# Modulations of a two-layer token mixer: a 32-column zero-padded left operand, pieces of 512 columns over four column groups, one ScalarE copy out

## The chip, the cores and the metric

The kernel runs on one core of a Trainium2 chip. The metric is the device time of one execution in microseconds (us); the lower the better. Five engines work in parallel, each through its own list of instructions in order: TensorE (PE for its matmuls, PEld for its weight loads), VectorE (DVE), ScalarE (ACT), GpSimd (POOL) and SyncE (SP), which here issues the DMA transfers.

## What is computed

Two layers over 1024 latent tokens and 256 context tokens of width 1024. Each layer mixes tokens by four groups of heads (mLSTM, Hyena, retention, RWKV), then by a convolutional feed-forward network, and both are modulated: six vectors of 1024 for latents and six for context come from one matrix product with a 1024 x 6144 matrix.

```
for l in range(DEPTH):
    mod = jnp.split((silu_c @ ada_w[l] + ada_b[l])[:, None, :], 6, axis=-1)
    modc = jnp.split(silu_cc @ ada_w[l] + ada_b[l], 6, axis=-1)
    ...
    u = modulate(layer_norm(x), mod[0], mod[1])
    uc = modulate(layer_norm(xc), modc[0], modc[1])
    y, y_c = token_mixer(u, uc, p, ang, not last)
    x = layer_norm(DEEPNORM_ALPHA * x + mod[2] * y, ln1_g[l], ln1_b[l])
    u = modulate(layer_norm(x), mod[3], mod[4])
    f = conv_ffn(u, ffn_w_up[l], ffn_conv_w[l], ffn_conv_b[l], ffn_w_down[l])
    x = layer_norm(DEEPNORM_ALPHA * x + mod[5] * f, ln2_g[l], ln2_b[l])
    ...
```

The last layer needs no context output. All arithmetic is in 32-bit floats; the large projections split an operand into a high and a low part (`uh`, `ul`) and use three matmuls.

## The kernel before, in words

The program is written as one stream. A scheduler sorts each engine's instructions, and pools with named buffers (tags) decide what must wait: a tile that takes a tag's buffer waits for the last user of the tile that had it.

**Modulations.** `sc` [128, 8, 2] holds the two activated vectors, eight blocks of 128 rows, one column for latents and one for context. It is the left operand (the loaded weights, two columns), the columns of the matrix are the right one. `ada` does the first two modulations of layer 0 in the setup: tiles of 128 x 1024 in six buffers, and four column groups of the array, 256 columns each, whose two result rows stand at rows 0, 32, 64 and 96 of a PSUM bank. `ada_steps` does the other four of layer 0 and the first two of layer 1 during layer 0's scan, and the last four of layer 1 during its scan: pieces of 256 columns over two column groups (40 pieces, 24 and 16), each with four tiles of 256 rows, two buffers. The loads of the next piece are written behind the matmuls of one, so two of its four tiles are prefetched. `ada_out` copies the two rows of each column group to `ab` on DVE (L940), transposes `ab` on PE (L941) and adds the bias to give columns of `modc` (L944).

**The scan.** `rwkv` runs ten steps of a chunked scan, both directions at once. `rwkv_prep` makes a step's operands (L484 to L541), `rwkv_inverse` inverts its triangular blocks by substitution (a transpose into the tile LM at L550, then 31 rounds on POOL and DVE, L557 and L558), `rwkv_tail` finishes the inverse (L565 to L591), `rwkv_chain` carries the state (L601 to L637). In step s the order in the text is inverse(s+1), chain(s), for some steps `group_norm` of two finished token tiles, tail(s+1), prep(s+2). The norm runs for s = 1 (layer 0 alone) and s = 6 to 9: sums on DVE (L651 to L653), a Square on ScalarE into its work space `gq` (L654), a sum of it (L655), square root (L656), reciprocal (L657), a product on POOL into `gq` (L658), and a store of `gq` to `yw` (L659). mLSTM runs beside the scan, with the modulations' pieces between its steps; its `keys` loads have three buffers.

**The setup and the front.** `tile_backbone` computes two modulations, then normalizes and modulates the ten input tiles; `to_u` transposes them and splits them (`uh`, `ul`, the last part on POOL, L1010). `filters` builds Hyena's filters: a feature table `fft` (L268), two small layers with a Sine (L273 to L280), products with a window (L287 to L139). Then come the projections with Hyena between them, and retention, whose state chain `rSS` runs on POOL (L826, L827) before its last part on PE.

Of the kernel before, what the change touches and what calls it, by code (L numbers as in the profile page):

```python
# [20 lines left out]
def rwkv_consts():  # L21
# [6 lines left out]
    c['rwmask']=np.stack([mf,mb],1)          # [128,2,128]  # L28
# [10 lines left out]
def mr_consts():  # L39
# [3 lines left out]
    mk=np.zeros((128,2,128),np.float32)   # [j,dir,i]  # L43
    mk[:,0]=np.where(i[:,None]>i[None,:],-1e30,0); mk[:,1]=np.where(i[:,None]<i[None,:],-1e30,0)
    c['mmask']=mk
    # selection for token-major gathers: rows 0-7 wi, 32-39 wk, 64-71 em ; cols (dir,12)
# [5 lines left out]
    # decay broadcast: lhsT [8,(ft,dir),128]  # L52
# [5 lines left out]
    # block-diagonal rows [8 rows,(dir) , h', i]  # L58
# [26 lines left out]
def dft_consts(L):  # L85
    """two-stage real DFT of length 2L, n=128*n1+n2, k=R*m+r, R=2L/128"""
# [10 lines left out]
    F0=np.zeros((128,4,64))   # re0, reH, im0(row0=nyquist), imH  # L97
    F0[:,0]=np.cos(a0);F0[:,1]=np.cos(aH);F0[:,2]=-np.sin(a0);F0[:,2,0]=(-1.0)**n2;F0[:,3]=-np.sin(aH)
    I0=np.zeros((128,4,128))  # B0 from re, B0 from im, BH from re, BH from im
# [36 lines left out]
class Eng:  # L136
    """elementwise ops on DVE or on Pool"""
    def __init__(s,nc,pool): s.nc=nc; s.e=nc.gpsimd if pool else nc.vector; s.pool=pool
    def tt(s,out,a,b,op): s.e.tensor_tensor(out=out,in0=a,in1=b,op=op)  # L139
    def axpy(s,out,a,sc,b,op=ALU.add,tmp=None):   # a*sc op b  # L140
# [5 lines left out]
def stage_a(K,E,x,H,CW,ptag):  # L146
    """x: view [128,H,CW] (n1 = token tile). returns accessor re(r), im(r) for r=0..H"""
# [29 lines left out]
def fwd_slot(K,cs,dst_re,dst_im,slot,H,pre,pim,qre=None,qim=None):  # L177
    """matmuls of one slot: re part from (pre,pim), im part from (qre,qim)"""
# [10 lines left out]
def fft_conv(K,Ksp,x,out,H,CW):  # L189
    """x view [128,H,CW], Ksp DRAM AP [128,H,2,CW]; out callback(par(0/1), AP [128,H//2,CW] time values)"""  # L190
# [18 lines left out]
    BB=p.tile([128,2*H,CW],F32,tag="hE",name="BB")   # re r -> r (0..H), im r -> H+r  # L209
# [20 lines left out]
    # g: [128, comp(re,im), r, par, CW]  # L230
# [10 lines left out]
    # a4: even +re B4, odd -im B4  # L241
# [14 lines left out]
def hyena_filter(K,l,L,Ksp):  # L256
    """Ksp DRAM tile [2 order][128,H,2,256]"""
# [89 lines left out]
def seg_conv(k,dst,src,w,ctx=True):  # L347
    """three-tap conv of a padded feature-major tile; w = (prev, mid, next, bias) columns"""
# [18 lines left out]
def kparts(k,D,ft,t,kk):  # L367
    """keys (or normalized keys) to the groups of wrk: r | k of even heads, kk of odd ones | the other way round | kk"""
# [7 lines left out]
def rwkv_front(k,l,pv,pvr,last):  # L376
    """projections, token shift, key normalization, gate and bonus of the RWKV group"""
# [52 lines left out]
def rwkv(K,l,pv,last,p1,p2,p3):  # L430
    """Chunked scan, 64 tokens a chunk, both directions at once, two chunks of each a step.  Even heads keep (b,SA,S) on partitions
    0-63 and (k,V) on 64-127, odd heads the other way round."""
# [229 lines left out]
def mlstm(K,l,GT,last,side=None):  # L662
# [13 lines left out]
    def keys(t):  # L676
        kT=p.tile([128,2,128],F32,tag="mk",name="mk",bufs=3)
        nc.sync.dma_start(kT,K.D['mqk'][256:512,t*128:t*128+128].rearrange("(f p) t -> p f t",p=128))
        return kT
# [765 lines left out]
```

## Time and profile before

| what | us |
|---|---|
| runs of the kernel, median of 3 | 4327.93 |
| lowest and highest of them | 4318.99, 4331.74 |
| profiled execution, its span | 4332.8 |

The profiled execution's own time is given by its span alone; it lies 4.9 us above their median. The sums further down are made against the span and then taken to the runs. A count of busy time says what an engine did, and not that something waited for it; that is read from the timeline and from waits.

### The profile page before, as it was taken

Reading aid. Unit: us, or ns where it says so; the run is one execution under the profiler, and the core shown is the slowest. Engines: PE = TensorE matmul, PEld = TensorE weight load, DVE = VectorE, ACT = ScalarE, POOL = GpSimd, SP = SyncE. Lnnn points to the kernel's source line nnn. Section 1 sums busy time; section 2 is a strip of 40 time slices with the busy share of each in tenths; the row PEclk is TensorE's granted clock in tenths of the full one; section 3 lists DMA queues with packets and bytes.
Section 4 is the critical chain, followed back from the end, with each engine's and each line's share of the span. In section 5 each row is a group of like instructions: output and inputs, shape, how many; then the busy total and the mean of one; then the engine's idle time right before and its main releaser. Section 6 shows DMA issues by size and latency. Waiting matters only on the chain.

```text
span 4332.8 us, 65427 instructions
## 1 busy us (share of the span) xinstructions
PE 3976.9 (92%) x24976; PEld 3226.9 (74%) x24976; DVE 2644.4 (61%) x5384; ACT 1462.4 (34%) x2909; POOL 1094.6 (25%) x2204
## 2 busy tenths in 40 slices
PE   6999999689979999999996899997899879999997
PEld 3878877566657888888884688885666758888885
DVE  5656665889766544444448555776889664444446
ACT  4333233554344211111124443344544342112112
POOL 3230023566535000000033330033666340000004
PEclk6999999799989999999998999996899789999999
DMA  4235553444343111111113235553333331111112
GB/s 164 72 102 173 158 152 110 114 145 121 116 134 122 45 39 35 44 40 35 38 36 114 83 103 153 171 160 96 123 111 102 125 102 54 45 43 54 44 49 97
DMA packets 477141, 414.18 MB, mean 96 GB/s; under 512 B 48827, under 2 KB 443285, under 8 KB 474011
## 3 DMA queue, kind: packets, MB, share of 16 engines
q1 hardware_dynamic: 476826, 409.99, 31.1%
q8 instruction: 197, 3.23, 0.3%
q14 instruction: 118, 0.96, 0.1%
HBM read 323.65 MB, written 86.25 MB: 95 GB/s over the span
## 4 chain that ended last, share of the span: by engine, by line
PE 49%; DVE 11%; ACT 3%; issue 3%; DMA 3%; POOL 3%; SPq 0%; POOLq 0%; ACTq 0%; DVEq 0%
PE bank L1021 8%; PE bank L1023 8%; PE bank L1022 8%; PE dbank L1021 6%; PE dbank L1022 6%; PE dbank L1023 6%; DMA xt<-x 1%; DVE bst L983 1%; POOL ul L1157 1%; DVE facc L1204 1%; PE bank L186 1%; PE bank L187 0%; DMA wst<-in_w_out 0%; DVE G L530 0%; DVE XL L558 0%
## 5 line engine op out<-in xcount | busy, mean ns | idle before, releaser
L1021 PE MATMUL dbank<-uh,wh 128*128 128x512 f32 (+1 forms) x2120 | 764.4, 370 | 9.5 <-ACT tmpB L398 5.5
L1022 PE MATMUL dbank<-ul,wh 128*128 128x512 f32 (+1 forms) x2120 | 760.0, 368 | 0.0
L1015 DVE TENSOR_TENSOR wl<-wst,wh 128x1024 fp32r<-128x1024 f32 x146 | 188.9, 1295 | 491.4 <-ACT wh L1014 342.0
L1023 PE MATMUL dbank<-uh,wl 128*128 128x512 f32 (+1 forms) x2120 | 480.9, 367 | 0.0
L1021 PEld LDWEIGHTS dbank<-uh,wh 128*128 128x128 f32 x2120 | 401.1, 189 | 85.8 <-ACT ztok L1113 6.1
L1022 PEld LDWEIGHTS dbank<-ul,wh 128*128 128x128 f32 x2120 | 401.3, 189 | 68.4 <-issue 0.8
L1023 PEld LDWEIGHTS dbank<-uh,wl 128*128 128x128 f32 x2120 | 366.2, 188 | 70.6 <-issue 1.1
L1232 POOL MEMSET fz<- 128x1 f32 x132 | 7.3, 99 | 1441.4 <-DVE fc L1247 1441.2
L1021 PE MATMUL bank<-uh,wh 128*128 128x512 f32 (+1 forms) x920 | 337.8, 375 | 11.4 <-ACT uh L1009 11.4
L1263 DVE TENSOR_TENSOR facc<-facc,bank 128x512 f32<-128x512 f32 x324 | 222.1, 687 | 204.8 <-PE bank L1023 204.8
L1022 PE MATMUL bank<-ul,wh 128*128 128x512 f32 (+1 forms) x920 | 337.9, 375 | 4.1 <-POOL ul L1010 3.6
L1021 PE MATMUL bank<-wdh,gh 128*128 128x512 f32 x792 | 315.2, 400 | 19.2 <-DVE facc L1277 11.1
L1022 PE MATMUL bank<-wdl,gh 128*128 128x512 f32 x792 | 310.5, 392 | 3.4 <-DVE wdl L1015 3.4
L1023 PE MATMUL bank<-wdh,gl 128*128 128x512 f32 x792 | 248.7, 393 | 0.0
L1014 ACT ACTIVATE wh<-wst 128x1024 fp32r<-128x1024 f32 x146 | 154.6, 1059 | 226.2 <-PE dbank L1022 157.7
L1014 ACT ACTIVATE wdh<-wst 128x1024 fp32r<-128x1024 f32 x46 | 48.7, 1061 | 524.8 <-PE bank L1023 427.8
L557 POOL TENSOR_TENSOR lt<-LM,XL 128x48 f32<-128x48 f32 (+26 forms) x620 | 187.4, 302 | 121.7 <-ACT XL L551 51.1
L558 POOL TENSOR_TENSOR XL<-XL,lt 128x48 f32<-128x48 f32 (+26 forms) x620 | 205.9, 332 | 47.8
L1023 PE MATMUL bank<-uh,wl 128*128 128x512 f32 (+1 forms) x920 | 212.6, 373 | 0.0
L1021 PEld LDWEIGHTS bank<-uh,wh 128*128 128x128 f32 x920 | 176.2, 192 | 42.9 <-ACT uh L1009 12.2
L1022 PEld LDWEIGHTS bank<-ul,wh 128*128 128x128 f32 x920 | 176.0, 191 | 36.1 <-POOL ul L1010 4.3
L1021 PEld LDWEIGHTS bank<-wdh,gh 128*128 128x128 f32 x792 | 149.9, 189 | 59.2 <-DVE facc L1277 11.9
(480 smaller groups left out, 8283.0 us busy)
## 6 DMA issues: line engine op xcount, KB each, us to landing
wst<-in_ffn_w_up SPq DMA_DIRECT2D x88, 512.0 KB
adaw<-in_ada_w SPq DMA_DIRECT2D x160, 256.0 KB
wst<-in_w_in SPq DMA_DIRECT2D x58, 512.0 KB
wst<-in_ffn_w_down SPq DMA_DIRECT2D x46, 512.0 KB
df<-in_c_F SPq DMA_DIRECT2D x10, 1344.0 KB
xt<-x SPq DMA_DIRECT2D x26, 512.0 KB
df<-in_c_I SPq DMA_DIRECT2D x8, 1344.0 KB
rkk<-wrk SPq DMA_DIRECT2D x10, 1024.0 KB
```

The lines of the kernel that those rows point to most:

```text
L186: mm(dst_re,F[:,i],pre(slot),start=True,stop=False); mm(dst_re,F[:,i+1],pim(slot),start=False,stop=True)
L557: e.tensor_tensor(out=t_,in0=LM[:,j,j+1:32].unsqueeze(2).to_broadcast([128,n,m]),in1=X[h][:,j:j+1,0:m].to_broadcast([128,n,m]),op=A.mult)
L558: e.tensor_tensor(out=X[h][:,j+1:32,0:m],in0=X[h][:,j+1:32,0:m],in1=t_,op=A.add)
L983: for h in range(2): nc.vector.bn_stats(out=st[:,h],in_=x[h])
L1014: k.nc.scalar.activation(out=h,in_=st,func=ACTF.Copy)
L1015: k.nc.vector.tensor_tensor(out=lo,in0=st,in1=h,op=ALU.subtract)
L1021: mm(ps,lh,rh,start=(i==0),stop=False)
L1022: mm(ps,lh,rl,start=False,stop=False)
L1023: for i,((lh,ll),(rh,rl)) in enumerate(pairs): mm(ps,ll,rh,start=False,stop=(i==n-1 and more is None))
L1157: nc.gpsimd.tensor_tensor(out=k.ul[:,fs,c],in0=yT,in1=k.uh[:,fs,c],op=ALU.subtract)
L1204: e[0].tensor_tensor(out=y,in0=y,in1=g,op=ALU.mult)
L1263: else: tt(out=d,in0=d,in1=ps,op=ALU.add)
```

## The change

1. `ada_sc` makes a left operand of 32 columns a block: `sc` in the first two, zeros in the others. It is made in the setup and in each layer's scan. The matmuls write 32 rows of each column group, so all 128 rows of a bank where four groups are used.
2. `ada_steps` has pieces of 512 columns over four column groups (20 pieces, 12 and 8), each with eight tiles of 128 rows by 512 columns, still two buffers. A tile has 256 KB as before; there are 160 loads and 640 matmuls (1280 records) as before.
3. `ada_out` makes one ScalarE copy of all rows, and each piece has one transpose of 128 rows and one add.
4. RWKV's group norm takes its work space from the tag of LM, which has one buffer, instead of a tag of its own.
5. mLSTM's `keys` have two buffers instead of three.

```
-            group_norm(K,YF[:,sl],K.D['yw'].rearrange("(t p) c -> p t c",p=128)[:,sl],2,p2.tile([128,8,64],F32,tag="gq",name="gq"),"gnw")
+            group_norm(K,YF[:,sl],K.D['yw'].rearrange("(t p) c -> p t c",p=128)[:,sl],2,p2.tile([128,16,64],F32,tag="LM",name="gq"),"gnw")
...
-        kT=p.tile([128,2,128],F32,tag="mk",name="mk",bufs=3)
+        kT=p.tile([128,2,128],F32,tag="mk",name="mk",bufs=2)
...
+def ada_sc(k,pool):
+    s=pool.tile([128,8,32],F32,name="scz"); k.nc.gpsimd.memset(s,0.0); k.nc.gpsimd.tensor_copy(out=s[:,:,0:2],in_=k.sc)
+    return s
...
-    for j in range(G): nc.vector.tensor_copy(out=ab[32*j:32*j+2],in_=ps[32*j:32*j+2,0:n])
+    nc.scalar.activation(out=ab,in_=ps[:,0:n],func=ACTF.Copy)
...
-        for i in range(4): nc.tensor.matmul(b[32*i:32*i+2,0:256],k.sc[:,q],w[:,i*256:i*256+256],start=(q==0),stop=(q==7))
+        for i in range(4): nc.tensor.matmul(b[32*i:32*i+32,0:256],sc[:,q],w[:,i*256:i*256+256],start=(q==0),stop=(q==7))
...
-    nc=k.nc; units=[(l,g*1024+p*256) for l,g in todo for p in range(4)]; w={}
-    bias=ada_bias(k,todo,pool); ab=pool.tile([64,128],F32,name="ab"); nc.gpsimd.memset(ab,0.0)
+    nc=k.nc; units=[(l,g*1024+p*512) for l,g in todo for p in range(2)]; w={}
+    bias=ada_bias(k,todo,pool); ab=pool.tile([128,128],F32,name="ab"); sc=ada_sc(k,pool)
     def load(u):
         l,c0=units[u]; w[u]=[]
-        for h in range(4):
-            t=pool.tile([128,2,256],F32,tag="adaw",name="adaw",bufs=2); w[u].append(t)
-            nc.sync.dma_start(t,k.a['ada_w'][l,h*256:h*256+256,c0:c0+256].rearrange("(q p) c -> p q c",p=128))
+        for q in range(8):
+            t=pool.tile([128,512],F32,tag="adaw",name="adaw",bufs=2); w[u].append(t)
+            nc.sync.dma_start(t,k.a['ada_w'][l,q*128:q*128+128,c0:c0+512])
...
-                for j in range(2): nc.tensor.matmul(ps[32*j:32*j+2,0:128],k.sc[:,q],w[u][q//2][:,q%2,j*128:j*128+128],start=(q==0),stop=(q==7))
+                for j in range(4): nc.tensor.matmul(ps[32*j:32*j+32,0:128],sc[:,q],w[u][q][:,j*128:j*128+128],start=(q==0),stop=(q==7))
...
```

The scheduler sorts the changed program anew. Lines of the changed kernel from `ada_out` on are numbered six higher. DVE has 5278 instructions instead of 5386, ScalarE 2927 instead of 2911, PE 19342 instead of 19362.

DVE in layer 1's scan, around the transpose of inversion 8 (counted from 0) into LM. Before, its rows from the end of inversion 7 (the transpose of its result XL, L565) to that of LM:

```order
L565 STREAM_TRANSPOSE T_29958<-XL 128x128 [waits Pool_49]
L569 STREAM_TRANSPOSE XT_25622<-T_29958 32x4x32 [waits DVE_49]
L569 STREAM_TRANSPOSE XT_25622<-T_29958 32x4x32
L571 STREAM_TRANSPOSE AX<-T_29958 32x128
L569 STREAM_TRANSPOSE XT_25622<-T_29958 32x4x32
L940 COPY ab<-mbank 2x128 [waits PE_49]
L940 COPY ab<-mbank 2x128
L569 STREAM_TRANSPOSE XT_25622<-T_29958 32x4x32
L571 STREAM_TRANSPOSE AX<-T_29958 32x128
L550 STREAM_TRANSPOSE LM<-NB 128x1024 [waits Activation_49]
```

Of the change, the same engine's last rows ahead of the same transpose (the end of inversion 7, L565, stands 71 instructions ahead of it):

```order
L617 COPY VSA<-cbank 64x128 [waits Activation_49]
L655 TENSOR_REDUCE gn_r<-gq 128x8 [waits Activation_49]
L657 RECIPROCAL gn_r<-gn_r 128x8 [waits Activation_49]
L624 TENSOR_TENSOR SV<-cbank,rho 64x128 [waits PE_49]
L624 TENSOR_TENSOR SV<-cbank,rho 64x128
L657 RECIPROCAL gn_r<-gn_r 128x8 [waits Activation_49]
L785 TENSOR_TENSOR NUM<-NUM,mbank 128x260 [waits PE_49] x2
L624 TENSOR_TENSOR SV<-cbank,rho 64x128 [waits PE_49]
L624 TENSOR_TENSOR SV<-cbank,rho 64x128
L550 STREAM_TRANSPOSE LM<-NB 128x1024 [waits DMAHW1_49,Pool_49]
```

The chain of step 6 (SV, VSA) and its norm (gn_r) have moved ahead of the transpose, which now waits for a DMA and for POOL. The DMA is the store of gq.

SyncE's queue in the setup, around the load of the filter's feature table `fft`. Before, it stands behind two loads of input tiles, ahead of the window's (wn):

```order
L953 DMA adaw<-in_ada_w 128x1024 [waits DMAHW0_49,PE_49]
L1420 DMA xt<-in_x 128x1024 [waits DMAHW1_49]
L1420 DMA xt<-in_x 128x1024 [waits DMAHW2_49]
L268 DMA fft<-in_c_FT 33x1024 [waits DMAHW3_49]
L288 DMA wn<-in_c_WIN 128x128 [waits DMAHW4_49]
```

Of the change, it stands behind the last loads of the input (the two context tiles) and six of the biases:

```order
L1426 DMA xt<-in_ctx 128x1024 [waits DMAHW5_49,PE_49]
L1426 DMA xt<-in_ctx 128x1024 [waits DMAHW6_49,PE_49,Activation_49]
L884 DMA rowst<-in_ada_b 8x128 [waits PE_49]
L884 DMA rowst<-in_ada_b 8x128 [waits DMAHW0_49]
L884 DMA rowst<-in_ada_b 8x128 [waits DMAHW1_49]
L884 DMA rowst<-in_ada_b 8x128
L884 DMA rowst<-in_ada_b 8x128 [waits DMAHW3_49]
L884 DMA rowst<-in_ada_b 8x128 [waits DMAHW4_49]
L268 DMA fft<-in_c_FT 33x1024 [waits DMAHW6_49,DMAHW5_49,Pool_49]
```

The load of fft moved behind all ten input tiles and waits for POOL, which it did not before.

PE in layer 0's scan, where its first modulation piece begins. Before (adaw are the tiles of the matrix):

```order
L973 MATMUL mbank<-adaw,sc 2x128 [waits PE_49]
L973 MATMUL mbank<-adaw,sc 2x128 x3
L973 MATMUL mbank<-adaw,sc 2x128 [waits DMAHW5_49]
L973 MATMUL mbank<-adaw,sc 2x128 x3
L492 MATMUL pbank<-TWA,W_6721 128x128 [waits DMAHW7_49,Activation_49]
L492 MATMUL pbank<-TWA,W_6721 128x128 x2
```

Of the change, in the same place:

```order
L979 MATMUL mbank<-adaw,scz 32x128 [waits PE_49]
L979 MATMUL mbank<-adaw,scz 32x128 x3
L979 MATMUL mbank<-adaw,scz 32x128 [waits DMAHW5_49]
L979 MATMUL mbank<-adaw,scz 32x128 x3
L733 MATMUL mbank<-ident,mk 128x128 [waits DMAHW5_49,DVE_49,PE_49]
L733 MATMUL mbank<-ident,mk 128x128
L979 MATMUL mbank<-adaw,scz 32x128 [waits DMAHW1_49]
L979 MATMUL mbank<-adaw,scz 32x128 x3
L979 MATMUL mbank<-adaw,scz 32x128 [waits DMAHW2_49]
L979 MATMUL mbank<-adaw,scz 32x128 x3
```

A tile still feeds four matmuls, but now one block of rows in four column groups instead of two blocks in two; a piece has eight such groups of four, with other work between some of them.

## Rows read from the trace of the kernel before

**Rows 1.** The page: busy us, share of the span, instructions.
```profile
PE 3976.9 (92%) x24976; PEld 3226.9 (74%) x24976; DVE 2644.4 (61%) x5384; ACT 1462.4 (34%) x2909; POOL 1094.6 (25%) x2204
```

**Rows 2.** Table by stretch: us, then PE, PEld, DVE, ACT, POOL busy.
```profile
101.00:706.00 605.00, 592.31 (x3511) 501.51 (x3510) 369.81 (x773) 217.92 (x437) 116.71 (x244) 0.99 0.44 130
...
804.00:1127.00 323.00, 290.84 (x3407) 216.02 (x3408) 282.79 (x885) 152.76 (x440) 209.40 (x595) 0.88 0.39 117
```

**Rows 3.** Timeline of DVE and POOL, both scans: start us, us, operation.
```profile
804.50 1.95 DVE L550 STREAM_TRANSPOSE LM<-NB 128x1024 f32<-128x1024 f32 x1
...
908.21 1.95 DVE L550 STREAM_TRANSPOSE LM<-NB 128x1024 f32<-128x1024 f32 x1 [0.96 <-POOL lt L557]
...
908.25 0.20 POOL L558 TENSOR_TENSOR XL<-XL,lt 128x4 f32<-128x4 f32 x1
...
1126.92 1.97 DVE L550 STREAM_TRANSPOSE LM<-NB 128x1024 f32<-128x1024 f32 x1
...
3351.32 1.92 DVE L550 STREAM_TRANSPOSE LM<-NB 128x1024 f32<-128x1024 f32 x1
```

**Rows 4.** Groups by line: ns min/median/max, first and last start, forms.
```profile
L940 DVE COPY ab<-mbank x80: 236/282/284, 846.0 to 3335.4; 2x128 f32<-2x128 f32 x80
...
L614 ACT ACTIVATE U<-cbank x80: 250/278/307, 851.0 to 3412.4; 128x128 f32<-128x128 f32 x80
```

**Rows 5.** Timeline of PE (a scan piece, the setup), then groups by line.
```profile
840.60 0.61 PE L973 MATMUL mbank<-adaw,sc 128*2 128x128 f32 x8
...
8.86 4.45 PE L954 MATMUL dbank<-adaw,sc 128*2 128x256 f32 x40
...
L973 PE MATMUL mbank<-adaw,sc x1280: 271/272/421, 837.2 to 3331.8; 128*2 128x128 f32 x183
...
L1078 PEld LDWEIGHTS dbank<-uh,wh x24: 107/107/170, 95.4 to 106.3; 128*32 128x32 f32 x24
```

**Rows 6.** Waits of PE in layer 0's scan: us in total, times, longest.
```profile
PE mbank L973 <- DMA adaw<-in_ada_w: 6.0, 6, 2.4
```

**Rows 7.** The chain that ended last, in layer 1's scan.
```profile
3178.54 2.81 DMA adaw<-in_ada_w
```

**Rows 8.** Timeline of SyncE's queue: stores of RWKV's normalized output.
```profile
1151.51 0.37 SPq L659 DMA_DIRECT2D yw<-gq  x1
...
1209.77 0.37 SPq L659 DMA_DIRECT2D yw<-gq  x1
...
3379.56 0.39 SPq L659 DMA_DIRECT2D yw<-gq  x1
...
3421.20 0.36 SPq L659 DMA_DIRECT2D yw<-gq  x1
```

**Rows 9.** Timeline of ScalarE: the reader of the last store.
```profile
3423.43 1.06 ACT L1156 ACTIVATE uh<-yT 128x1024 fp32r<-128x1024 f32 x1 [3.61 <-DMA yw<-gq]
```

**Rows 10.** Timeline of POOL in the setup, then its groups by line.
```profile
100.67 2.40 POOL L1010 TENSOR_TENSOR ul<-tum,uh 128x1024 fp32r<-128x1024 f32 x1
...
L139 POOL TENSOR_TENSOR pq<-hh x16: 445/450/639, 83.0 to 105.2; 128x128 f32<-128x128 f32 x16
...
L139 POOL TENSOR_TENSOR hh<-hh,wn x8: 717/724/727, 81.6 to 103.0; 128x256 f32<-128x256 f32 x8
```

**Rows 11.** Groups by line, 0 to 101, then 101 to 706: busy, mean.
```profile
L287 PE MATMUL bank<-fw,fh 64*128 64x128 f32 x32 | 8.3, 438 | 2.2 <-ACT fh L280 2.2
...
L273 PE MATMUL bank<-fft,fw 33*64 33x512 f32 x4 | 3.7, 1071 | 1.4 <-DMA fft<-in_c_FT 1.4
...
L820 PE MATMUL bank<-rqkv,k 128*128 128x64 f32 x76 | 9.4, 269 | 0.0
```

**Rows 12.** Timeline of POOL: memsets and retention's state chain.
```profile
706.05 0.55 POOL L435 MEMSET W<- 128x512 f32 x1 [11.48 <-PE dbank L1023]
...
713.37 1.83 POOL L452 MEMSET XT<- 128x1024 f32 x2
...
724.61 1.86 POOL L827 TENSOR_TENSOR rSS<-rSS,rst 64x256 f32<-64x256 f32 x1
```

More of the change, by code (lines that the diff above doesn't have):

```diff
@@ L945, in ada_out, with ada @@
         in1=tv(bias[l,m][:,j0:j0+G*e].unsqueeze(2).to_broadcast([128,G*e,2])),op=ALU.add)
-def ada(k,l,g,pool,ab,loads,bufs,bias):
+def ada(k,l,g,pool,ab,loads,bufs,bias,sc):
     nc=k.nc; b=k.dbank()
@@ L1413, in tile_backbone @@
         loads=[]
-        ab=pa.tile([128,256],F32,name="ab"); nc.gpsimd.memset(ab,0.0)
+        ab=pa.tile([128,256],F32,name="ab"); sc=ada_sc(k,pa)
         bias=ada_bias(k,[(0,0),(0,1)],pa)
-        for g in range(2): ada(k,0,g,pa,ab,loads,6,bias)
+        for g in range(2): ada(k,0,g,pa,ab,loads,6,bias,sc)
         mc=k.modc[:,0:2].rearrange("p m j s -> p s m j")
```

## The prediction

> **What bounds the kernel now.** I read the page's busy shares first, since they name the engine that could gain: TensorE (PE) is busy 92% of 4332.8 us, VectorE (DVE) 61% [rows 1]. A share is a mean over stages, so the table by stretch comes next. From 101 to 706 us lie layer 0's projections, with PE busy 592.31 of 605 us; from 804 to 1127 its scan, where no engine is full: PE 290.84 and DVE 282.79 of 323 us [rows 2]. Layer 1's scan is alike and ends its tenth inversion after 3351.32 [rows 3]. The modulations run in the setup, before 101, and in both scans. What paces a scan is a chain: each of ten steps has an inversion, 62 short operations on GpSimd (POOL) and 30 on DVE, and the next one's first instruction, the transpose into LM, starts as the one before ends. The reader sees it in the timeline of the two engines: POOL's last operation of an inversion stands at 908.25, the next transpose at 908.21. Ten transposes from 804.50 to 1126.92 make a period of 35.8 us [rows 3].
>
> **The change, part by part.**
>
> *Copies, adds, transposes.* DVE's 80 copies of 0.282 us (22.6 us) become 20 copies on ScalarE [rows 4]; the nearest ScalarE row, a PSUM copy of 128x128, takes 0.278, so 5.6 us on an engine busy 152.76 of 323 [rows 2, 4]. The adds fall from 40 to 20, PE's transposes too. DVE loses some 26 us, three fifths in layer 0. These are rows of DVE and counted in the scan term below, not again.
>
> *TensorE.* In the scan eight records of a piece take 0.61 us, each 0.272: two column groups at once, so a pair starts every (0.61-0.27)/3 = 0.113 us. In the setup, where four groups are used already, 40 longer records end in 4.45 us, 0.111 each for twice the columns: far less than one record's length, so they do run side by side [rows 5]. The 1280 scan records then cost 320 x 0.113 = 36 us in place of 640 x 0.113 = 72; PE loses 22 us in layer 0, 14 in layer 1. The padded operand is 32 columns wide; a weight load of that width takes 0.107 us elsewhere [rows 5], less than the matmul beside it, on a queue busy 216.02 of 323 [rows 2]. I take nothing for PE, as it isn't in the chain of inversions; that it is, is a rival.
>
> *Refills.* A piece now has 8 tiles instead of 4, with two buffers: three pairs of loads behind the prefetched one instead of one, 60 rounds instead of 40. PE waited 6.0 us in six waits on them in layer 0's scan, which had 24 of the 40 [rows 6]: 0.25 a round, so **+5** for twenty more. Upper bound: nothing else stands between and each waits for a whole landing, 2.81 us in the chain that ended last [rows 7]: +56. The order puts scan matmuls between most rounds, which is nearer to the first. The Trainium skill, page "DMA: Bandwidth & Descriptors", section "Anatomy of one DMA — SWDGE (gpsimd) path", speaks against this part: about 2.0 us for every transfer, mostly its completion, plus bytes/436e3 us. It describes another queue than this one; for 256 KB an estimate from that page is 2.6 us, and twenty uncovered rounds would cost 52 us instead of 5. The landing in the chain has nearly that length; the sum of PE's waits shows that most of it is covered.
>
> *The group norm's work space.* It now shares the single buffer of LM. So the Square of step s's norm must wait for the end of inversion s+1, and the transpose of inversion s+2 for the norm's store to land. The order confirms it: transposes 3, 8 and 9 of layer 0 (counted from 0) and 8 and 9 of layer 1 now wait for a DMA. Before, the stores that transposes 9 must now follow were issued at 1151.51 and 3379.56, and these transposes started at 1126.92 and 3351.32, 24.6 and 28.2 us ahead [rows 3, 8]. What fills the gap is the tail, the chain and the norm of one step and the preparation of another, all in series with the inversion now. Counting DVE's instructions in the order, from an inversion's end to the next transpose: layer 0's nine gaps held 122 and now 245 (70, 66 and 20 in the three, where there were 8, 16 and 3); layer 1's 107 and now 221 (71 and 25, where there were 9 and 9). Inside the inversions they fall from 761 to 689 and from 780 to 699.
>
> A DVE instruction costs 323/885 = 0.365 us at the scan's pace [rows 2]. *By pace:* between the first and the last transpose layer 0 has 51 more, +18.6 us, layer 1 33 more, +12.0. Each of the five transposes also waits for its store: 3421.20 to the start of the reader of the last one at 3423.43, 2.23 us, and the issue's 0.36 [rows 8, 9], +7.8 and +5.2. The stage behind the last transpose has less left: 195 instructions ahead of the last norm's reciprocal become 116, and 162 become 89. At 0.365 that is 28.8 and 26.6 us, but an inversion, a tail, a chain and a norm remain in series there: layer 1's 70 us (3351.32 to 3421.20) against layer 0's 83 (1126.92 to 1209.77) [rows 3, 8], for 33 fewer, show how far it shrinks. I take -15 and -5. Together +11.4 and +12.2. *By the floor:* instructions that leave an inversion shorten it only as long as DVE, not POOL's own 62 in a row, is what it waits for. They are worth 72 x 0.365 = 26.3 and 81 x 0.365 = 29.6 us. If half of that isn't realised: +24.5 and +27.0. I take +18 for each layer, between the two: **+36**. Bounds: -25 (store waits covered, end stages giving back 28.8 and 26.6) and +52.
>
> *Front of layer 0.* The padded operand takes 1 KB of each partition in the setup's pools, and by the pools' offsets the filter's feature table now overlaps a buffer of the input tiles. The order shows its load on SyncE's queue behind both loads of context tiles, waiting for POOL; POOL's last product of the input starts at 100.67 [rows 10]. So the filter comes after the input. The input then ends sooner, since its products on POOL no longer alternate with the filter's (16 of 0.45 and 8 of 0.72 between 82 and 105, 13 us, all but the last before 103 [rows 10]): I take 11 us. The projections start that much earlier, take in 8.3+3.7+3.7 us of filter matmuls (two of the groups are alike) at the setup's low clock, some 7 at full, and give off 9.4 us of retention's [rows 11], because Hyena, whose filter is late, holds retention back until after the last projection: -13. Retention's state chain on POOL ended at 726.47, 20.4 after the stage's end; it must then run whole behind POOL's memsets, 706.05 to 715.20: nine us and 32 operations of some 0.8, 35 after it: +15 [rows 12]. Net **+2**, from -13 (the chain stays covered) to +17 (the setup gains only what the filter costs).
>
> *Sum.* +5 +36 +2 = +43 on 4332.8, so 4376; that execution lies 4.9 us above the median of 4327.93, so in terms of runs **4371**.
>
> **The rivals.** *Faster:* the scan is paced by throughput after all, PE being busy for 90% of it [rows 2]. Then 36 us of matmuls and some 5 of transposes leave, nine tenths of that from the time, -37; queued work fills the waits for the stores; with the +7 from elsewhere 4298. For it: both engines are nearly full. Against: a transpose starts with the inversion's end, though PE still has waits there. It decides if the five gaps cost less than 24 us beyond what the inversions lose. *Same:* the work is only moved, and the end stages give back all: 18.6+7.8-28.8 = -2.4 and 12.0+5.2-26.6 = -9.4, with +7: 4323. Against: an end stage in series. *Refills uncovered:* +56 in place of +5: 4422, above the range; for it the landing in the chain, against it six waits of 6.0 us. *The change does not do what it says:* four groups side by side might want more than this; but the setup's rows show them, and as PE isn't in the sum it would cost nothing here.
>
> **How the numbers follow.** A measurement of this kernel tells about 0.3%, 13 us, from no change: the bounds are 4315 and 4341. The forecast case, slower, has 4341 to 4402: down to a third of the scan term, up to +52 in the scans with +17 and +5 (4402). It gets 0.57; refills uncovered 0.08, so slower 0.65. Same has 0.17: two arguments, pace and floor, must both be too high. Faster has 0.18, as PE's share is the one number that fits it. Leaving out the uncovered refills and most of the faster case, the range is 4312 to 4402.
>
> **What would show it.** Right: LM's transposes 3, 8, 9 and 8, 9 end a wait for the norm's store, with POOL idle for 20 to 30 us ahead of the 3, 8 and 8 and for about 10 ahead of the two 9; the other periods near 32 us; the stage behind the last transpose shorter. No copies of two rows on DVE, 20 on ScalarE, four records starting every 0.113 us on PE. The feature table loaded after 80 us, the input's last product near 90, retention's state chain behind the last projection. Wrong: gaps ahead of 3, 8 and 8 that leave POOL idle for less than 15 us, or a scan whose other periods shrink under 30, so that inversions were paced by shared engines; waits for modulation loads above 20 us a layer; a scan of layer 0 that starts at 755 or earlier.

## The result and the profile after

The changed kernel takes 4371.57 us (median of 4 runs, 4365.06 to 4384.66) against 4323.46 of the kernel before in the same sessions; the ratio is 1.0116 [1.0093, 1.014]. The forecast was 4371, slower. The profiled execution has a span of 4363.3 us, its run took 4365.06. The ratio is not the quotient of the two medians and can differ from it, by up to 0.0022 in the runs below; where that matters both are given. The total was right, and two of its terms, the front and layer 0's scan, were not; this section shows where the time stands, the next one takes the change apart.

First the table by stretch of the changed kernel, with the columns of [rows 2]: us, busy time of PE, PEld, DVE, ACT and POOL with counts, granted clock of TensorE (1.00 is the upper of its two levels, 2.4 GHz, 0.50 the lower), DMA share, GB/s. The stretches are the projections, three parts of retention, and the ten inversions of each layer's scan.

```profile
87.00:687.00 600.00, 590.87 (x3468) 494.56 (x3466) 348.82 (x751) 217.06 (x430) 91.90 (x226) 0.99 0.44 130
687.00:716.00 29.00, 18.75 (x88) 16.19 (x88) 27.12 (x48) 6.43 (x17) 27.33 (x36) 0.69 0.37 117
716.00:740.00 24.00, 13.45 (x81) 11.00 (x79) 10.95 (x15) 4.23 (x8) 21.89 (x28) 0.78 0.28 87
740.00:799.00 59.00, 58.27 (x252) 52.24 (x251) 16.78 (x38) 15.39 (x33) 4.17 (x4) 0.50 0.05 17
840.00:1220.00 380.00, 332.13 (x3943) 246.64 (x3943) 309.28 (x935) 173.20 (x490) 217.26 (x604) 0.85 0.41 126
...
3048.00:3410.00 362.00, 306.80 (x3497) 231.09 (x3497) 304.14 (x921) 168.94 (x488) 212.47 (x599) 0.81 0.36 112
```

The projections end 18.9 us sooner than before (687.0 against 705.9), but what was retention's tail of 58 us is now 112: a stretch in which DVE and POOL are both full (27.12 and 27.33 of 29), POOL's chain (21.89 of 24), and a last part in which PE is busy for nearly all of its time (58.27 of 59 us) at the half clock. The kernel before, in the same view, had 0.71 beside the chain and 0.93 behind it:

```profile
706.00:726.00 20.00, 13.75 (x80) 11.32 (x78) 14.61 (x23) 4.37 (x9) 18.87 (x26) 0.71 0.44 131
726.00:764.00 38.00, 37.79 (x262) 31.77 (x261) 18.92 (x42) 15.67 (x33) 4.05 (x5) 0.93 0.16 56
```

Cut finer, the kernel before was at 0.50 as well when its chain ended, from 716 to 731 us; from 731 to 764 it had 0.99, and 253 matmul records took 33 us there. In the changed kernel the 252 records of the same lines take the 59 us at 0.50. What stood between in the kernel before is a group of six wider matmuls (first line), which the changed kernel ran some 13 us ahead of the chain's end (second line):

```profile
726.15 4.58 PE L422 MATMUL dbank<-tmpA,bones 128*128 128x512 f32 x6
...
724.27 2.42 PE L422 MATMUL dbank<-tmpA,bones 128*128 128x512 f32 x6 [1.73 <-DVE tmpA L418]
```

The timeline of the setup and of retention in the changed kernel (start us, us, engine, line, operation) answers to [rows 10, 12]:

```profile
84.63 2.40 POOL L1016 TENSOR_TENSOR ul<-tum,uh 128x1024 fp32r<-128x1024 f32 x1 [1.39 <-ACT uh L1015]
...
87.06 0.29 SPq L268 DMA_DIRECT2D fft<-in_c_FT  x1
...
689.22 10.79 POOL L812 TENSOR_TENSOR rtmp<-rqkv,crsin 128x128 f32<-128x128 f32 x16 [1.14 <-issue]
...
701.35 6.14 POOL L450 MEMSET AR<- 64x1024 f32 x6
...
738.42 1.51 POOL L827 TENSOR_TENSOR rSS<-rSS,rst 64x256 f32<-64x256 f32 x2
```

The feature table is loaded right after the last product of the input, which ends at 87.03 instead of 103.07. Behind the last projection POOL then has, in this order, the rotations of retention's rows (L812), the memsets, and the chain, which ends at 739.93.

The timeline of layer 0's scan, around inversion 8, and its end, answers to [rows 3, 8]; the first line is one group of modulation matmuls, for [rows 5]:

```profile
875.60 0.43 PE L979 MATMUL mbank<-adaw,scz 128*32 128x128 f32 x8
...
1119.77 1.92 DVE L550 STREAM_TRANSPOSE LM<-NB 128x1024 f32<-128x1024 f32 x1
...
1152.64 0.20 POOL L558 TENSOR_TENSOR XL<-XL,lt 128x4 f32<-128x4 f32 x1
...
1179.24 0.36 SPq L659 DMA_DIRECT2D yw<-gq  x1
...
1181.54 1.97 DVE L550 STREAM_TRANSPOSE LM<-NB 128x1024 f32<-128x1024 f32 x1 [0.27 <-DMA yw<-gq]
...
1203.38 0.15 DVE L950 TENSOR_TENSOR modc<-mbank,adab 128x8 f32<-128x8 f32 x1
...
1228.01 0.36 SPq L659 DMA_DIRECT2D ym<-gq  x1
...
1275.21 0.38 SPq L659 DMA_DIRECT2D yw<-gq  x1
...
1278.57 0.79 PE L1027 MATMUL bank<-wo,uh 128*128 128x512 f32 x1 [4.21 <-ACT uh L1162]
```

Inversion 7 ends at 1152.84, the next transpose waits for the norm's store and starts 28.7 us later: a period of 61.8 us in place of 35.8. RWKV's last store (`yw`) is followed by the output projection after 3.4 us; mLSTM's (`ym`) was issued 47 us before it. In the kernel before it was the other way round; this is a stretch of its timeline that the rows ahead of the prediction left out:

```profile
1212.40 0.15 DVE L944 TENSOR_TENSOR modc<-mbank,adab 128x4 f32<-128x4 f32 x1
...
1222.67 0.36 SPq L659 DMA_DIRECT2D ym<-gq  x1
...
1242.30 0.77 PE L1021 MATMUL bank<-wo,uh 128*128 128x512 f32 x1 [20.34 <-ACT uh L1156]
```

There RWKV's last store was issued at 1209.77 [rows 8], and the output projection began 32.5 us later, behind the last modulation (1212.40), mLSTM's last norm (its store at 1222.67) and the weights loaded after that. So layer 0's scan stage is ended by the later of two streams: RWKV's, and that of mLSTM with the modulations between its steps. This holds in all thirteen kernels of this document: in four the output projection starts 3.3 to 3.4 us behind RWKV's last store, in the nine others 19 to 24 us behind mLSTM's, as long as the weights take. Before, the second one was later by 29 us (32.5 less 3.4).

The groups by line for the new copies and matmuls, then the waits of PE on modulation loads, layer 0's scan stage (800 to 1280) first, layer 1's (3005 to 3470) behind it, answer to [rows 4 to 6]:

```profile
L946 ACT ACTIVATE ab<-mbank x20: 250/277/278, 887.3 to 3347.7; 128x128 f32<-128x128 f32 x20
...
L979 PE MATMUL mbank<-adaw,scz x1280: 269/297/423, 864.7 to 3345.9; 128*32 128x128 f32 x183
```

```profile
PE mbank L979 <- DMA adaw<-in_ada_w: 14.8, 15, 4.1
...
PE mbank L979 <- DMA adaw<-in_ada_w: 9.0, 11, 2.3
```

From such timelines the span of the first seven kernels is cut into five stages, at the first transpose into LM of each layer's scan and at the first matmul of each output projection (us, one profiled execution each; before: 804.5, 1242.3, 3028.5, 3424.5, 4332.8):

| kernel | to scan 0 | scan 0 to output | to scan 1 | scan 1 to output | rest |
|---|---|---|---|---|---|
| before | 804.5 | 437.8 | 1786.2 | 396.0 | 908.3 |
| changed | 839.9 | 438.7 | 1769.7 | 415.1 | 899.9 |
| before, norm in LM | 803.9 | 443.9 | 1772.3 | 415.7 | 902.5 |
| before, 1 KB tile | 846.2 | 433.1 | 1792.4 | 400.1 | 907.9 |
| changed, own norm buffer | 843.8 | 429.9 | 1767.3 | 395.4 | 904.7 |
| changed, small ab | 801.5 | 437.5 | 1768.8 | 416.7 | 908.7 |
| changed, both cures | 805.3 | 406.0 | 1771.8 | 405.6 | 904.7 |

### The profile page after: what moved, and what is told of

The parts are those of the page before. It is cut to its first block, busy times and chain, and to the rows that moved or that the text cites. A ratio compares the mean times of both kernels' runs of the same rounds, so it can differ in the third digit from the quotient of the medians.

```text
span 4363.3 us, 65337 instructions
## 1 busy us (share of the span) xinstructions
PE 3970.1 (91%) x24956; PEld 3227.0 (74%) x24956; DVE 2591.0 (59%) x5276; ACT 1457.9 (33%) x2925; POOL 1094.2 (25%) x2207
```

## The experiments

The first four separate three parts of the change: the shared norm buffer, the 1 KB that moves addresses in the setup, and the modulations' new form.

**The norm's buffer alone.** The kernel before with one edit:

```
-... p2.tile([128,8,64],F32,tag="gq",name="gq"),"gnw")
+... p2.tile([128,16,64],F32,tag="LM",name="gq"),"gnw")
```

> The kernel before with one thing changed: the group norm's work space is taken from LM's buffer. Theory A (the shared buffer is a main part of the loss): transposes 3, 8, 9 of layer 0 and 8, 9 of layer 1 wait for the norm's store as in the changed kernel, the two 8s start some 25 us late; from the first transpose to the first matmul of the output projection layer 0 is 0 to 15 us longer, since the weights of that projection then load in the gap, and layer 1 about 19; the kernel 10 to 35 us slower, at about 4345. Rival B (the loss is in the new pieces of the modulations, their refills and the ScalarE copy): within 5 us of the kernel before. The start of layer 0's scan stays at 804 by both.

Measured: 4327.22 against 4322.62 us, ratio 1.0007 [0.9988, 1.0026]. By the time of the whole it was rival B's outcome; by the stages it was not. Its timeline around transpose 8 of layer 0 and at the output projection:

```profile
1072.04 1.94 DVE L550 STREAM_TRANSPOSE LM<-NB 128x1024 f32<-128x1024 f32 x1 [0.29 <-ACT NB L536]
...
1130.00 0.37 SPq L659 DMA_DIRECT2D yw<-gq  x1
...
1133.05 1.95 DVE L550 STREAM_TRANSPOSE LM<-NB 128x1024 f32<-128x1024 f32 x1
...
1247.78 0.79 PE L1021 MATMUL bank<-wo,uh 128*128 128x512 f32 x1 [4.81 <-ACT uh L1156]
```

The gap is there (a period of 61.0 us), layer 1's scan stage is 19.7 us longer, layer 0's only 6.1: its lateness went into the 32 us that the output projection waited for the other stream anyway. That the whole came out equal is in part another matter, a 14 us shorter stretch ahead of scan 1, where the kernel before had a half clock in its profiled execution (last part of the next section).

**The 1 KB alone.** The kernel before with an unused tile, and the memset of it, beside the setup's:

```
         ab=pa.tile([128,256],F32,name="ab"); nc.gpsimd.memset(ab,0.0)
+        pad=pa.tile([128,256],F32,name="pad"); nc.gpsimd.memset(pad,0.0)
```

> The kernel before with an unused tile of 1 KB a partition beside the setup's tiles, so that nothing but addresses changes. Theory A: the filter's feature table is loaded behind all input tiles (about 83 us instead of 20), the last projection of layer 0 ends near 687 to 693 instead of 706, retention runs behind it, and the first transpose of layer 0's scan stands at about 839 if retention's last part runs at the half clock, at about 818 if it runs at the full one; the kernel 12 to 35 us slower. Rival B (the padded operand's cost lies elsewhere): the first transpose stays within 5 us of 804 and the time within 5 us.

Measured: 4370.06 against 4322.62 us, ratio 1.0088 [1.0061, 1.0116]: by the medians 47 us, nearly as much as the whole change, by the ratio 38 (26 to 50). The table by stretch shows the same retention as in the changed kernel, at the half clock at its end:

```profile
694.00:722.00 28.00, 18.41 (x91) 15.90 (x90) 27.82 (x47) 6.73 (x18) 25.81 (x39) 0.66 0.36 106
722.00:746.00 24.00, 15.15 (x76) 11.31 (x74) 12.74 (x17) 4.06 (x8) 21.79 (x26) 0.71 0.30 104
746.00:805.00 59.00, 58.41 (x255) 52.75 (x254) 16.88 (x38) 15.29 (x32) 4.17 (x4) 0.50 0.04 15
```

Theory A's links hold, with a loss at or above the top of its 12 to 35 us, and the front is the largest loss of the change.

**The norm's own buffer back.** The changed kernel with the tag `gq` again; to make room for it the scan's padded operand is taken from mLSTM's pool:

```
-... p2.tile([128,16,64],F32,tag="LM",name="gq"),"gnw")
+... p2.tile([128,8,64],F32,tag="gq",name="gq"),"gnw")
...
-    ... ab=pool.tile([128,128],F32,name="ab"); sc=ada_sc(k,pool)
+    ... ab=pool.tile([128,128],F32,name="ab"); sc=ada_sc(k,k.p_ml)
```

> The changed kernel with the group norm's own buffer given back; the scan's padded operand lies in mLSTM's pool to make room for it. Theory A: no transpose waits for a store, periods near 34 us or below with the lighter DVE and PE, the scans 0 to 15 us shorter each than before the change, the front still 35 us late: about 4345. Rival B (pieces and refills lose the time): scans as long as in the changed kernel, about 4370.

Measured: 4337.83 us, ratio to the kernel before 1.0025 [1.0009, 1.0042]. That is 34 us less than the changed kernel, so beside the new modulations the shared buffer costs far more than the 5 us that it cost alone.

**The setup's overlap undone.** The changed kernel with a tile `ab` of half the size, so that the addresses no longer overlap:

```
-    nc.scalar.activation(out=ab,in_=ps[:,0:n],func=ACTF.Copy)
-    for i in range(e): nc.tensor.transpose(t[:,i*G*32:(i+1)*G*32],ab[:,i*128:i*128+128],k.ident[0:G*32,0:G*32])
+    for i in range(e):
+        nc.scalar.activation(out=ab,in_=ps[:,i*128:i*128+128],func=ACTF.Copy)
+        nc.tensor.transpose(t[:,i*G*32:(i+1)*G*32],ab,k.ident[0:G*32,0:G*32])
...
-        ab=pa.tile([128,256],F32,name="ab"); sc=ada_sc(k,pa)
+        ab=pa.tile([128,128],F32,name="ab"); sc=ada_sc(k,pa)
```

> The changed kernel with the setup's ab tile halved (two copies of 128 columns in place of one of 256), so that the feature table no longer overlaps an input buffer. Theory A: the feature table is loaded at about 20 us again, the first transpose of layer 0 stands near 800, and retention's last part has the full clock; the kernel about 30 us faster than the changed one, near 4340. Rival B: within 8 us of the changed kernel.

Measured: 4331.42 us, ratio 1.0015 [0.9997, 1.0033]: 40 us less than the changed kernel. The feature table is loaded at 22.04 us again, retention's last part is at 1.00 from 730 us on, and the first transpose stands at 801.5.

**Both cures.**

> The changed kernel with both cures: the group norm's own buffer and the halved ab tile in the setup; what is left are the 32-column operand, the pieces of 512 columns, the ScalarE copy and two buffers for mLSTM's keys. Theory A, by the stages of the runs so far (layer 0's scan 5 to 8 us shorter than in the kernel before, layer 1's equal, the front equal): the front as in the kernel before, no transpose waits for a store, 4310 to 4320, that is 3 to 12 us under the kernel before. Rival B (the modulations' new form has a cost of its own, by its refills): at or above the kernel before, 4325 to 4335.

Measured: 4290.06 against 4320.88 us, ratio 0.992 [0.9893, 0.9947]: faster than both kernels, and 20 us under the lower end of theory A's 4310 to 4320. What is left of the change comes with a gain of 31 us. Of the 39 us between the two profiled executions 32 lie in layer 0's scan; 14 lie ahead of scan 1, where the kernel before had a half clock (below), and layer 1's scan is 10 longer. Its timeline at the end of scan 0:

```profile
1168.85 0.17 DVE L951 TENSOR_TENSOR modc<-mbank,adab 128x8 f32<-128x8 f32 x1
...
1211.29 0.79 PE L1028 MATMUL bank<-wo,uh 128*128 128x512 f32 x1 [13.85 <-ACT uh L1163]
```

The last modulation ends 44 us sooner than in the kernel before, and the output projection starts 31 us sooner, though RWKV's last store is only 6.7 us earlier (1203.1). With this kernel as the base the costs are plain: adding the shared buffer (small ab) 41 us, adding the setup's overlap (own norm buffer) 48, by the medians; -31 of the rest, 41 and 48 would give 4379 on 4321, and the change itself has 4372. The 48 are not the front's alone: by the table 38.5 lie there, 23.9 in layer 0's scan, -4.5 ahead of scan 1 and -10.2 in it. Why the overlap lengthens layer 0's scan beside the new pieces is not settled.

**The pieces of before, with the padded operand and the ScalarE copy.** The kernel with both cures, pieces of 256 columns over two groups:

```
-    nc=k.nc; units=[(l,g*1024+p*512) for l,g in todo for p in range(2)]; w={}
+    nc=k.nc; units=[(l,g*1024+p*256) for l,g in todo for p in range(4)]; w={}
...
-                for j in range(4): nc.tensor.matmul(ps[32*j:32*j+32,0:128],sc[:,q],w[u][q][:,j*128:j*128+128], ...
+                for j in range(2): nc.tensor.matmul(ps[32*j:32*j+32,0:128],sc[:,q],w[u][q//2][:,q%2,j*128:j*128+128], ...
```

> The kernel with both cures, but with the pieces of before: 256 columns over two column groups, four tiles of 256 rows a piece, one refill round a piece; the 32-column operand and the ScalarE copy (now 40 copies of 64 rows) stay. Theory D (layer 0's scan ends with the mLSTM and modulation stream, and the new pieces shorten that stream by their matmuls): from layer 0's first transpose to its output projection some 430 us instead of 406, the last modulation add near 400 us behind that transpose instead of 364, the kernel 4310 to 4320. Rival E (the gain is VectorE's relief by the ScalarE copy): as with both cures, within 6 us of 4290.

Measured: 4302.62 us, ratio 0.9943 [0.9921, 0.9965], 13 us above the kernel with the new pieces and 21 under the kernel before. Scan 0 to output takes 433.9 us, as theory D said, and scan 1 to output 397.1, less than the 405.6 of the new pieces. The last modulation and the output projection of layer 0:

```profile
1208.03 0.11 DVE L951 TENSOR_TENSOR modc<-mbank,adab 128x4 f32<-128x4 f32 x1
...
1237.52 0.77 PE L1028 MATMUL bank<-wo,uh 128*128 128x512 f32 x1 [20.08 <-ACT uh L1163]
```

So the 28 us in layer 0's scan come from the pieces, as D said; the time of the whole is lower than D's 4310, and of the 21 us against the kernel before only 4 stand in that scan. A rival is the new order of the whole program. It doesn't explain the sign: from the first transpose to mLSTM's last store the seven kernels with the old pieces take 413 to 422 us, four of the five with the new ones and two buffers 386 to 391, and the fifth (own norm buffer, front still late) 406. Whether the pieces save by their matmuls or by half as many copies, transposes and adds wasn't separated, and the operand, the ScalarE copy and mLSTM's two `keys` buffers were not tried one by one.

**One buffer for the modulations' tiles**, `bufs=1` in place of 2, in the kernel with both cures.

> The kernel with both cures, and one buffer instead of two for the modulations' tiles of 256 KB, so that each of the 160 loads waits for the matmuls before it. If refills are exposed at their full landing time of some 2.8 us, TensorE's waits on these loads rise by 200 us or more, and with them the two scans. If other streams fill them (as the prediction took it, 0.25 us a round), the waits rise to 40 to 60 us and the kernel is 0 to 15 us slower than with two buffers.

Measured: 4394.6 us, ratio 1.0159 [1.013, 1.0187], 105 us above two buffers. Neither number fits: PE's waits on these loads rise only from 7.7 to 29.7 us in layer 0 and from 9.7 to 12.1 in layer 1, and yet scan 0 to output takes 511.8 us. RWKV's last store is at 1188.0, sooner than with two buffers; it is the other stream that is late:

```profile
1286.21 0.16 DVE L951 TENSOR_TENSOR modc<-mbank,adab 128x8 f32<-128x8 f32 x1
...
1316.57 0.76 PE L1028 MATMUL bank<-wo,uh 128*128 128x512 f32 x1 [19.80 <-ACT uh L1163]
```

The added 106 us are 1.1 us for each of that layer's 96 loads, and PE's waits show a fifth of them. It fits that RWKV's matmuls filled the waits; in any case the price stands in the stream's own length, which ends the stage, and not in PE's idle time.

**Filling TensorE beside retention's chain.** Four kernels test the half clock, with extra matmuls whose results nothing uses. In the first (the kernel before with the 1 KB tile, layer 0):

```
             nc.gpsimd.tensor_tensor(out=SS[q,nx],in0=SS[q,nx],in1=tmp[q],op=A.add)
+            if l==0:
+                b=K.bank()
+                for h in range(8): mm(b[:,0:256],K.ident,SS[:,nx].rearrange("p a d -> p (a d)"),start=True,stop=True)
```

> The kernel before with the unused 1 KB tile, and in layer 0 extra matmuls on TensorE between the steps of retention's state chain (64 of 256 columns, their results are used by nothing). Theory A (22 us of the late retention are its last part at the half clock, after TensorE stood half idle beside the chain): the last part has a granted clock near 0.95 and takes 38 us instead of 60, the first transpose of layer 0 stands near 824 and the kernel is 15 to 22 us faster than with the tile alone, in spite of the added work. Rival C (the last part is longer for another reason, or the clock doesn't follow the work ahead of it): it stays at 60 us and the time is that of the tile alone or above.

Measured: 4383.49 us, ratio 1.0138 [1.0114, 1.0162], slower than the tile alone. The clock did what theory A said, the time did not: the last part takes 42 us at 1.00, but the filling made the chain wait for it (POOL stood idle for 22 us until its matmuls were done) and stood ahead of the last part, as the table by stretch shows (the chain and the filling, then the last part):

```profile
746.00:785.00 39.00, 38.68 (x182) 33.53 (x181) 0.00 (x0) 0.00 (x0) 9.41 (x14) 1.00 0.00 1
785.00:827.00 42.00, 41.33 (x323) 36.75 (x321) 20.58 (x46) 18.79 (x39) 3.44 (x4) 1.00 0.06 20
```

In the second the filling is lighter and reads states that are finished:

```
+                for h in range(3): mm(b[0:64,0:256],K.ident[q,q],SS[q,cur].rearrange("p a d -> p (a d)"),start=True,stop=True)
```

> The kernel before with the unused 1 KB tile, and lighter filling than in the run with 64 extra matmuls: 48 of 64 rows that read states which are already finished, so that the chain on GpSimd doesn't wait for them. Theory A (the last part of retention is slow by the half clock, which follows TensorE's idling beside the chain): if the filling is enough to keep the clock, the last part takes some 40 us instead of 60, the first transpose stands near 828, and the kernel is 10 to 18 us faster than with the tile alone, 4352 to 4360. If the clock falls all the same: no gain, 4370 to 4380, and the last part again 60 us.

Measured: 4349.44 us, ratio 1.0049 [1.003, 1.0068], by the medians 21 us under the tile alone, by the ratios 17. The first transpose stands at 824.7 instead of 846.2. The chain, then the last part:

```profile
722.00:750.00 28.00, 23.10 (x158) 16.33 (x154) 9.50 (x14) 3.47 (x7) 18.86 (x25) 0.92 0.23 71
750.00:784.00 34.00, 33.95 (x264) 30.28 (x263) 17.31 (x40) 15.41 (x33) 3.42 (x4) 1.00 0.07 24
```

With PE busy 23 of 28 us beside the chain the clock was 0.92 there, and the last part took 34 us at 1.00 instead of 59 at 0.50. Adding work to a half idle engine made the kernel faster, and that the half clock is what makes the last part long is shown. That idling alone brings it isn't (last section).

In the third and the fourth the condition `l==0` of the light filling becomes layer 1 alone, in the kernel before, and both layers, in the kernel with both cures.

> The kernel before with the light filling (48 matmuls of 64 rows whose results nothing uses) beside retention's state chain in layer 1 alone, where the profiled execution had its last part at a granted clock of 0.62 for 41 us, and seven of the other kernels of this study some 28 to 29 us at the full clock. If that part is slow in most executions of the kernel before: the last part takes 28 to 30 us and the kernel is 5 to 12 us faster, so that as much of the new modulations' gain in the profiled pair is a matter of the clock and not of their work. If it was slow in the profiled execution alone: no difference within 4 us.

Measured: 4320.34 against 4325.35 us, ratio 0.9985 [0.9973, 0.9997], some 5 us, at the low end of what was expected; the interval, 1 to 12 us, leaves room for the other case too. The last part ran at 1.00, but it didn't take 28 to 30 us: from the chain's end to the first transpose of scan 1 it was 79 us, where the kernel before had 81 and nine kernels at the full clock without this filling have 65 to 69. The filling had taken the place of retention's own matmuls beside the chain: 64 transposes (L835, L841) and 64 products (L849) were left behind it, where the kernel with both cures has 32 and 46. So the work that it displaced gave back most of what the clock gained. Of its 12 executions none took over 4327 us, where 8 of 23 of the kernel before took over 4330.

> The kernel with both cures and the light filling in both layers' retention. If the clock in retention is safe in the kernel with both cures already (0.93 or more in its last parts), the filling brings nothing or costs up to 5 us: 4288 to 4296. If some executions lose it, up to 10 us faster: 4280.

Measured: 4322.96 us, ratio 0.9993 [0.998, 1.0006], that is 33 us slower than without the filling. This was a plain miss. The clock was safe without the filling (1.00 in both last parts, in layer 0 after its first 10 us), and the displaced work costs as above: from the chain's end to the next scan it takes 89 us in layer 0 and 78 in layer 1, where the kernel with both cures has 79 and 67. By the stages layer 0's front is 7 and the stretch ahead of scan 1 15 us longer. The other 11 stand in scan 0 to output, 417.0 us instead of 406.0, where RWKV's last store comes 16 us later behind the first transpose; what moved it was not tried.

## Why the prediction came out, point by point

*The total, 4371, was right; the split was not.* By the table of stages the profiled pair differs by +35.4 (front), +0.9 (scan 0 to output), -16.5, +19.1 (scan 1) and -8.4: +30.5. The prediction had +2, +18, nothing, +18, and +5 for refills within the scans. The front was 33 us too low, scan 0 with its share of the refills 20 too high, scan 1 within 1, and two stages that had been put at nothing gave 16.5 and 8.4 us back. So the terms miss by 33, 20 and 25 us one against the other; by the medians of the runs, where the kernels differ by 48 us and not by 30, the sum of 43 came within 5. That 4371 was met is luck. The forecast of slower rested on the scans; had the front been left alone, the kernel would have been within 0.3% (the small ab's 1.0015).

*Front of layer 0, "+2".* The mechanism was right in each link, and it is shown by the unused tile. Mis-sized were its links: the input ended 16.0 us sooner (11 predicted), the last projection 18.9 (13), the chain ended 52.9 us after it (35), and the last part took 59 us, where I had left it at 37. Of the chain's missing 18 us, 13 are the rotations, which I didn't move along with retention's matmuls (POOL ends them at 700.0), and 5 the chain itself (709.27 to 739.93, 30.7 us where I had 26); the other 22 us are the half clock, for which the sum had no term. The light filling shows that TensorE's work ahead of the last part moves that clock. That in the kernel before the six wide matmuls at the part's start raised it fits the rows above and wasn't tried by itself. The upper bound of +17 was too low for the same reasons.

*The group norm's work space, "+36" for both scans.* The waits fell where predicted, on transposes 3, 8, 9 and 8, 9. The argument by pace failed: between the first and the last transpose it was +57.5 and +39.1 us (predicted 26.4 and 17.2 by pace), since the other periods didn't shrink: layer 0's six without a wait (40.8, 32.2, 31.2, 33.6, 42.1 and 38.8) have a mean of 36.5, where 35.8 was the mean of all before [rows 3] and I expected 32. The end stages gave back 27.5 and 20.0 us (15 and 5 taken). To RWKV's last store the net is +30.0 and +19.1. Layer 1's +18 was right. For layer 0 the step that failed is the point to which I counted: the last store of RWKV, and not the output projection, which stood 32.5 us behind it, for the other stream. In the changed kernel the streams moved against each other: from the first transpose to its last store RWKV's took 435 us instead of 405 and mLSTM's 388 instead of 418, so the stage kept its 438. The two streams account for the buffer's price in either case: alone it moves that store by 35.3 us from the first transpose on (1244.4-803.9 against 1209.8-804.5), and 29.1 us of slack vanish (32.5 to 3.4), which leaves 6.1; beside the new modulations it moves it by 36.4 (1235.7-801.5 against 1203.1-805.3), and only 4.9 of slack vanish (8.2 to 3.3), which leaves 31.5. These are the stage's differences in the table.

*TensorE, "I take nothing".* The size was near (eight records in 0.43 us, each 0.297, so groups of four start 0.13 us apart; 0.113 predicted). That nothing hung on it was wrong: in layer 0 the modulations set the end of mLSTM's stream, which ended the stage. With both cures the new pieces are worth 28 us there. The faster rival, about 4298, went by TensorE's throughput; the kernel with both cures has 4290, by the end of a stream and not by throughput, and whether by PE's 36 us of matmuls wasn't separated.

*Refills, "+5".* PE's waits rose from 10.0 to 14.8 us in layer 0's scan stage and from 0.3 to 9.0 in layer 1's: +13.5, above the forecast and far from the 52 to 56 of full landings. The Trainium skill, page "DMA: Bandwidth & Descriptors", section "Anatomy of one DMA — SWDGE (gpsimd) path", has a fixed cost of about 2.0 us a transfer, by which an estimate for 256 KB was 2.6. The trace doesn't bear it out as the price of a round: the longest single wait is 4.1 us, and the sum is a quarter of twenty such transfers. The run with one buffer shows that such waits of PE are the wrong measure.

*What the other stages have, and what is open.* The stretch ahead of scan 1 takes 1767 to 1774 us in nine of the thirteen kernels and 1783 to 1792 in four. The difference is layer 1's retention, from the end of its chain to the scan's first transpose: 65 to 69 us in the nine, all at 1.00 behind the chain; 81 in the kernel before and 86 with the 1 KB tile, both at the half clock for most of it; 79 and 78 in the two with filling there. In the kernel before the last part had 0.62:

```profile
2947.00:2988.00 41.00, 39.74 (x203) 35.61 (x200) 12.97 (x29) 12.12 (x25) 3.93 (x4) 0.62 0.09 32
```

So some 12 to 15 us by which the other profiled executions are shorter than that of the kernel before are this clock, and neither the pieces nor the buffer. In how many executions of the kernel before it falls there isn't on record. Of the 21 us by which the kernel with the pieces of before is faster, up to 15 are explained by it and 4 by scan 0. Open is why scan 1, whose stage the new pieces lengthen by 8.5 us with both cures, is as long as before with the norm's own buffer alone (395.4), and the 8.4 us of the last stage.

## What to carry to other kernels

Count a stage to the first instruction that needs all of its streams, not to the end of the stream that is changed: where another ends later, a loss is hidden and a gain elsewhere is worth its full size. A tile of 1 KB that no one reads can cost more than the work that is being tuned, when it moves an address onto a buffer that another stage is to use; look at what the order of loads does after any change of sizes. And test the parts of a change one by one even if the sum fits: here it fitted for the wrong reasons, and two small cures turned 1.1% slower into 0.8% faster.

## What the runs showed of the hardware

TensorE's granted clock behind a thin stretch: with PE busy 13.45 of 24 us beside the chain, a part in which it was then busy for 58.27 of 59 us stayed at 0.50 to its end; with 23.10 of 28 us beside the chain (light filling) the same part had 1.00 and took 34 us. A count of busy time ahead does not tell the level by itself. In layer 0 the kernel before had 13.75 of 20 us ahead and 0.50 at the part's start, then six matmuls of 128x512 in 4.58 us and 0.99 behind them. In layer 1 it had 35.7 of 44 us beside the chain and 0.50 from 9 us behind it on, and the kernel with both cures 34.0 of 42 us and 1.00.

Eight 128x128 matmul records over four column groups end in 0.43 us, in place of 0.61 over two. A record is 0.297 us long at the median in the changed kernel and 0.272 before [rows 5]; with weights of 32 columns in two groups (the pieces of before) it is 0.273, so the width alone doesn't lengthen it.
